# Half-turn of an 8192 x 8192 matrix by DMA alone: 128 rows a DMA in place of 32

## The chip, the cores and the metric

The kernel runs on one core of one Trainium2 chip. It computes nothing: it only issues DMAs that copy from one tensor in the chip's HBM (its main memory) to another. The core has 16 DMA engines that move the bytes, and two queues from which this kernel feeds them: the SP queue, filled by SyncE (SP), and the ACT queue, filled by ScalarE (ACT). In the profile's list of queues they are q1 (SP) and q10 (ACT).

The metric is the device time of one execution in microseconds (us), the median of several runs. A profile of one execution shows when each DMA was issued, when it landed, and how busy the DMA engines were.

## The reference

```python
x = np.random.randn(8192, 8192).astype(np.float32)
out = np.fft.ifftshift(x)
```

For even sizes this swaps the halves in both directions: `out[r, c] = x[(r + 4096) % 8192, (c + 4096) % 8192]`. The upper half of the rows changes places with the lower half, and inside each row the left 4096 floats change places with the right 4096. A row is 8192 floats, 32 KB; half a row is 16 KB. The tensor is 268.44 MB; all of it is read once and written once.

## The kernel before, in words

Output rows are copied in blocks of 32 neighbouring rows (`rows`, line 29), one DMA of 1 MB a block, 256 DMAs in all. No data passes through on-chip memory.

One DMA is described by two access patterns. The source pattern (`read`, line 35) is 16 pieces, each 64 KB long: two whole rows (`wide`, line 28), which lie one behind the other in memory. The destination pattern (`write`, line 36) walks 32 rows, and in each row two pieces of 16 KB: first the right half (offset `hc`), then the left half (a step of `-hc`). The bytes are taken from the source in order, so the left half of a source row lands in the right half of the output row, and the other way round. The source block begins 4096 rows further on, modulo 8192 (line 33). With 16 pieces of source and 16 DMA engines, a DMA is one 64 KB read and four 16 KB writes for each engine; an engine has two neighbouring rows.

The order is written out by hand by the two loops at lines 47 to 50. The outer loop takes parts of 1024 rows (`part`, 32 MB). In a part the SP queue works through the first 512 rows and the ACT queue through the last 512, each in blocks of `rows` in increasing order; the program issues one to SP and one to ACT by turns. So at every time the two queues work about 512 rows (16 MB) apart, and each is given 128 DMAs.

The DMAs are independent of each other. The framework around the kernel (the Tile context) gives each DMA a completion semaphore out of eight, four for each queue in turn. A DMA on a queue is therefore issued only when the fourth one before it on that queue has landed: at most four DMAs per queue, eight in all, are under way. These waits stand at line 37, where the instruction is added. At the end SP waits for the last ones (line 76, in the launch code).

Of the kernel before, what the change touches and what calls it, by code (L numbers as in the profile page):

```python
# [1 line left out]

# [4 lines left out]


ENGINES = 16


@with_exitstack
def kernel(
    ctx: ExitStack,
    tc: tile.TileContext,
    x: bass.AP,
    out: bass.AP,
):

    nc = tc.nc
    R, C = x.shape
    hr = R // 2
    hc = C // 2
    wide = 2
    rows = ENGINES * wide
    part = 1024  # L30

    def copy(queue, name, row):
        src = x.offset + (row + hr) % R * C
        dst = out.offset + row * C + hc
        read = [[wide * C, ENGINES], [1, 1], [1, wide * C]]
        write = [[C, rows], [-hc, 2], [1, hc]]
        queue.add_instruction(
            mybir.InstDMACopy(
                name=nc.get_next_instruction_name(),
                queue=name,  # L40
                mode="Copy",
                ins=queue.lower_ap_dma(bass.AP(x.tensor, src, read)),
                outs=queue.lower_ap_dma(bass.AP(out.tensor, dst, write)),
            )
        )

    for first in range(0, R, part):
        for row in range(first, first + part // 2, rows):
            copy(nc.sync, "qSPDynamicHW", row)
            copy(nc.scalar, "qActDynamicHW", row + part // 2)  # L50


# [1 line left out]
_INS = ['x']  # L54
_OUTS = [((8192, 8192), 'float32')]


# [23 lines left out]
```

## Time and profile before

| what | value |
|---|---|
| median of 3 runs | 821.62 us (821.31 to 823.12) |
| the profiled execution, its own time | 821.65 us |
| its span, first to last instruction | 819.9 us |
| bytes | 268.44 MB read, 268.44 MB written |
| mean rate over the span, read and written together | 655 GB/s |
| DMAs | 128 on SP, 128 on ACT, 1024 KB each |
| from the issue of a DMA to its landing, median | 25.5 us |

The span leaves out what lies around the first and last instruction, here 821.65 - 819.9 = 1.75 us. The page cuts the span into 40 slices of 20.5 us and gives for each the busy share of the 16 DMA engines in tenths (9 means 90% or more) and the rate in GB/s. That rate counts each byte once, by the writes; the reads are the same again. A "packet" in the list of queues is one write or one completion message. The packets of 16 KB are the writes of half rows; those under 512 B are the completion messages, one per engine and DMA (256 x 16 = 4096). A share of the DMA engines can be printed a little above 1.00 in a short stretch, since a packet is counted whole where it begins.

### The profile page before, as it was taken

Reading aid. Unit: us, or ns where it says so; the run is one execution under the profiler, and the core shown is the slowest. Engines: PE = TensorE matmul, PEld = TensorE weight load, DVE = VectorE, ACT = ScalarE, POOL = GpSimd, SP = SyncE. Lnnn points to the kernel's source line nnn. Section 1 sums busy time; section 2 is a strip of 40 time slices with the busy share of each in tenths; the row PEclk is TensorE's granted clock in tenths of the full one; section 3 lists DMA queues with packets and bytes.
Section 4 is the critical chain, followed back from the end, with each engine's and each line's share of the span. In section 5 each row is a group of like instructions: output and inputs, shape, how many; then the busy total and the mean of one; then the engine's idle time right before and its main releaser. Section 6 shows DMA issues by size and latency. Waiting matters only on the chain. (4 is left out here: it accounts for less than half of the span.)

```text
span 819.9 us, 301 instructions
## 1 busy us (share of the span) xinstructions
POOL 0.2 (0%) x4
## 2 busy tenths in 40 slices
POOL 0000000000000000000000000000000000000000
DMA  9999999999999999999999999999999999999998
GB/s 301 329 327 330 323 331 333 323 333 330 325 333 331 331 329 324 333 332 327 331 328 329 331 329 334 329 332 328 333 320 325 330 328 333 327 335 326 329 325 294
DMA packets 20483, 268.47 MB, mean 327 GB/s; under 512 B 4097, under 2 KB 4097, under 8 KB 4097
## 3 DMA queue, kind: packets, MB, share of 16 engines
q1 hardware_dynamic: 10240, 134.23, 50.1%
q10 hardware_dynamic: 10240, 134.23, 49.3%
q14 instruction: 3, 0.02, 0.0%
HBM read 268.44 MB, written 268.44 MB: 655 GB/s over the span
## 5 line engine op out<-in xcount | busy, mean ns | idle before, releaser
L65 POOL MEMSET const-bfloat16-1.0<- 128x1 bf16 x1 | 0.1, 101 | 0.0
L65 POOL MEMSET const-uint8-127<- 128x1 uint8 x1 | 0.1, 101 | 0.0
L65 POOL MEMSET const-float32-0.0<- 128x1 f32 x1 | 0.1, 98 | 0.2 <-issue 0.2
L65 POOL MEMSET const-float32-1.0<- 128x1 f32 x1 | 0.1, 98 | 0.0
## 6 DMA issues: line engine op xcount, KB each, us to landing
out_dram<-in_x_dram ACTq DMA_DIRECT2D x128, 1024.0 KB, 25.5
out_dram<-in_x_dram SPq DMA_DIRECT2D x128, 1024.0 KB, 25.5
```

The costliest lines, as they stand in the source:

```text
L65: nc = _bacc.Bacc("TRN2", target_bir_lowering=False, num_devices=1)
```

## The change

A DMA covers 128 neighbouring rows in place of 32: 4 MB in place of 1 MB. The source pattern becomes 64 pieces of 64 KB, the destination pattern 128 rows of two halves. The size of a read (64 KB), the size of a write (16 KB), the two queues, the parts of 1024 rows, the order of rows and the framework's eight semaphores stay. There are 64 DMAs in place of 256, 32 on each queue; four blocks on each queue make up a part in place of sixteen.

```diff
     wide = 2
-    rows = ENGINES * wide
+    rows = ENGINES * 8
     part = 1024
 
     def copy(queue, name, row):
         src = x.offset + (row + hr) % R * C
         dst = out.offset + row * C + hc
-        read = [[wide * C, ENGINES], [1, 1], [1, wide * C]]
+        read = [[wide * C, rows // wide], [1, 1], [1, wide * C]]
         write = [[C, rows], [-hc, 2], [1, hc]]
```

If an engine is given a run of neighbouring pieces, it has four reads of 64 KB and sixteen writes of 16 KB a DMA: eight rows, 256 KB. The 16 engines then stand 256 KB apart in memory, where they stood 64 KB apart.

## The prediction

> **What bounds the kernel now.** I read the page from the top, then SP's waits, then the start, middle and end in stretches. First the page: span, slices, queues, issues.
>
> ```profile
> span 819.9 us, 301 instructions
> ...
> DMA  9999999999999999999999999999999999999998
> GB/s 301 329 327 330 323 331 333 323 333 330 325 333 331 331 329 324 333 332 327 331 328 329 331 329 334 329 332 328 333 320 325 330 328 333 327 335 326 329 325 294
> DMA packets 20483, 268.47 MB, mean 327 GB/s; under 512 B 4097, under 2 KB 4097, under 8 KB 4097
> ...
> q1 hardware_dynamic: 10240, 134.23, 50.1%
> q10 hardware_dynamic: 10240, 134.23, 49.3%
> ...
> out_dram<-in_x_dram ACTq DMA_DIRECT2D x128, 1024.0 KB, 25.5
> out_dram<-in_x_dram SPq DMA_DIRECT2D x128, 1024.0 KB, 25.5
> ```
>
> The two queues' packets take 50.1 + 49.3 = 99.4% of the time of 16 engines: the engines are full from end to end, and only their pace can change the time. The 38 inner slices average 329.1 GB/s and lie between 320 and 335. A write of 16 KB takes 0.994 x 16 x 819.9 us / 16,384 = 796 ns. The list of SP's waits comes next.
>
> ```profile
> SPq L37 <- DMA out_dram<-in_x_dram: 722.6, 124, 8.7
> ```
>
> SP waits 722.6 us before 124 of its 128 issues, each time for an earlier DMA to land. This is not the bound: with eight DMAs of 1 MB under way a landing must take 8 x 821.65/256 = 25.7 us, and it takes 25.5. The queue in front of the engines is never empty. Last the stretches: start, end, us, GpSimd (POOL), clock, share of the DMA engines, GB/s.
>
> ```profile
> 0.00:2.00 2.00, 0.20 (x4) 1.00 0.00 0
> 2.00:5.00 3.00, 0.00 (x0) 1.00 0.96 339
> ...
> 100.00:700.00 600.00, 0.00 (x0) 1.00 1.00 329
> ...
> 815.00:820.00 5.00, 0.00 (x0) 1.00 0.55 180
> ```
>
> Nothing moves for 2.0 us at the start, and in the last 5 us the engines are 45% idle (2.25 us). At 329.1 GB/s the 268.44 MB alone take 815.7 us; the other 821.65 - 815.7 = 5.95 us are these ends and what lies around the span. The median of the runs, 821.62, is the same as the profiled 821.65, so sums against the latter need no correction.
>
> **The change part by part.**
>
> *Fewer DMAs, so fewer seams.* 192 of 256 DMAs go, with three quarters of the completion packets. Idle time of the engines is 0.6% of 819.9 = 4.9 us; the ends explain 2.0 + 2.25 = 4.25, which leaves 0.65 us for all seams together. The completion packets also take engine time: 9 ns each in the packet records behind these views, 256 x 9 ns = 2.3 us per engine. Three quarters of both is 0.5 + 1.7 = 2.2 us. That is the most that can be gained here; the least is 0, because an engine held up by memory loses nothing by a 9 ns message. I take 0.5, the idle part alone.
>
> *Fewer issues.* An issue takes 553 to 560 ns, up to 820 at the start, in the durations of line 37; a queue's 128 of them make 71 us, all beside the transfers, since SP has 722.6 us to wait. Gain 0. If an issue grows with the number of pieces (four times 560 is 2.2 us), it is still hidden behind three DMAs of 4 MB on its queue. Only the first, 642 ns on ACT, is uncovered: 0 to 3 x 0.64 = 1.9 us. Issues of like size all take the same, so no row decides; I take 0, as the pieces can leave while the issue runs on.
>
> *The waits* go from 124 to 28 per queue, for landings four times as long (8 x 4 MB, some 103 us). Behind the waiting issue on SP and on ACT stand only later issues of the same queue. 32 MB are under way in place of 8, so no engine runs dry: 0.
>
> *The two ends.* The start's stretch is ACT's first DMA almost alone; SP follows. If ACT keeps its head start for sixteen writes an engine in place of four, SP is alone for as long at the end. One queue alone is not slower (339 GB/s in 2 to 5 us against 329), so 0. If the engines end four times as far apart, the 2.25 us idle at the end become 9: 0 to +6.8. I take 0: nothing makes an engine drift further because messages are rarer, as the waits do not hold the engines together now either.
>
> *The places in memory.* This is the term that decides. The 16 engines keep near step with each other. Now they stand 64 KB apart and cover one solid megabyte; afterwards they stand 256 KB apart over 4 MB. Sizes and order within an engine are the same. That memory, or the way to it, sets the pace can be seen: the same 16 KB write takes from 609 to over 1300 ns in the packet records, 796 on average. 0.61 us x 1024 writes per engine would be 625 us. So some 190 us are waiting, which the arrangement of addresses can raise or lower. No row shows another spacing. The nearest rows are the slices, which differ in address alone: the slowest, 320 GB/s, would make 838.9 us for the bytes (+23.2), the fastest, 335, 801.3 (-14.4). I take a loss: engines over one solid megabyte differ in every address bit from 64 KB up; at 256 KB they share two more bits at any moment, which can only put more of them on the same part of the memory, unless higher bits are mixed in. For its size I take the mean of the lower 19 slices, 326.4 GB/s: 822.4 us for the bytes, +6.7, since the extremes are single slices of 20.5 us.
>
> The Trainium skill bears on both sides. "DMA: Bandwidth & Descriptors", section "Measured (HBM→SBUF, 128 partitions, SWDGE, issued from GpSimd)", says to batch DMAs to at least 1 MiB and has larger ones faster still: 341 GB/s at 1 MB, 425 at 16 MB. By those two figures four times the size would, as an estimate from that page, gain up to a fifth; but they are loads into SBUF, and the share of 1.00 in the stretch from 100 to 700 us says that the fixed cost of a DMA is already covered here by the other seven. I give such a gain no more than what is left below the range. The same page, "Latency and other measured facts", reports copies between HBM tensors losing rate as the row pitch grows through large powers of two: 207 GB/s at 512 KiB, 103 at 4 MiB, against 214 with padding. Its lowest pitch is above our 256 KB; if the 3.4% between 214 and 207 held here, the estimate would be 849 us. No run so far shows which part of that table applies to engines 256 KB apart.
>
> The sum: 821.65 - 0.5 + 6.7 = 827.9, so 828.
>
> **The rivals.**
>
> *No effect of the places (821).* Only the seams count: 821.65 - 0.5 = 821.1, bounds 819.4 (all 2.2 gained) and 823.5 (a first issue four times as long). For it: the rate stays within 320 to 335 whatever rows are being copied, as if addresses were well mixed. Against it: even those slices differ by 4.6%, and all have the same spacing.
>
> *The places help (about 814).* This is the other side: with 190 us of waiting, if 16 engines side by side in one megabyte collide now, engines 256 KB apart collide less. At the mean of the upper 19 slices, 331.8 GB/s, the bytes take 809.0 and the whole 809.0 + 5.95 - 0.5 = 814.5; at 335 it is 806.8. It decides as soon as the rate passes 329.6 GB/s, where the sum is 0.2% below now. For it: the waiting is large. Against it: nothing shows that neighbours collide, and solid coverage is the more even spread.
>
> *The engines drift apart (828).* No change of pace, but the end stretched by 6.8 us and no gain at the seams that shows: 821.1 + 6.8 = 827.9. For it: each engine has 4 MB / 16 of its own to finish after the last issue. Against it: the last 5 us still have 55% of the engines busy, so they end close together though eight DMAs under way would allow 25 us.
>
> *The change does not do what it says.* The 64 pieces could be dealt one by one, so that engines stay 64 KB apart. Then only the seams are left: 821.1.
>
> **How the numbers follow.** Dearer places 0.42, forecast 828; drift 0.08; no effect 0.18 and pieces dealt one by one 0.06, both near 821; cheaper places 0.26. The runs of before differ by about 0.2% (1.6 us), which is also what a measurement of this kernel can tell from no change. Slower is 0.42 + 0.08 = 0.50. Of the 0.24 near 821, 0.03 fall below -0.2% by a full gain at the seams: same 0.21. Faster is 0.26 + 0.03 = 0.29. The range goes down to 808, about the fastest slice's 806.8, and up to 850: the slowest slice's 821.65 - 0.5 + 23.2 = 844 and most of a drift of 6.8 on top. The forecast's own range, of dearer places alone, is 823.5 to 850. Outside the whole range I leave 0.06 below and 0.09 above.
>
> **What would show it.** 64 issues of 4096 KB, landings of about 103 us, 28 waits on SP, 1024 completion packets and 16,384 writes: then the change is as described. The inner slices near 326 GB/s with the share of the engines still 9 in every slice: the places. Slices unchanged and a lower last one: the drift. Slices at 332 or more: the forecast is wrong because the waiting came from neighbours. Slices in the middle with a share under 9 would mean that engines ran dry, which no step here allows for.

## The result

| | before | after |
|---|---|---|
| median of 22 runs each | 821.82 us (820.97 to 823.12) | 822.99 us (822.01 to 824.14) |
| span of the profiled execution | 819.9 us | 821.4 us |

The ratio is 1.0014, with a 95% interval from 1.0008 to 1.0020. The kernel became 1.2 us slower: a real difference, but a fifth of the 6.3 us that was forecast, and below the 0.2% that the prediction counted as a change. It lies within the bounds of the rival "no effect of the places" (821.1, bounds 819.4 to 823.5).

The page after the change, the lines that answer to those of before:

```profile
span 821.4 us, 109 instructions
...
DMA  9999999999999999999999999999999999999999
GB/s 302 325 326 326 323 326 329 333 334 332 324 330 330 329 322 327 332 331 326 327 332 331 326 329 323 329 328 330 326 333 330 327 327 328 331 326 331 323 328 301
DMA packets 17408, 268.44 MB, mean 327 GB/s; under 512 B 1024, under 2 KB 1024, under 8 KB 1024
...
q10 hardware_dynamic: 8704, 134.22, 49.8%
q1 hardware_dynamic: 8704, 134.22, 49.7%
...
out_dram<-in_x_dram ACTq DMA_DIRECT2D x32, 4096.0 KB, 102.1
out_dram<-in_x_dram SPq DMA_DIRECT2D x32, 4096.0 KB, 102.0
```

By its counts the change did what it says: 64 issues of 4096 KB, 1024 completion packets, 16,384 writes, landings after 102 us where 103 were worked out. The engines are still full (49.8 + 49.7 = 99.5%). The inner 38 slices average 328.2 GB/s against 329.1, and lie between 322 and 334. That the engines now stand 256 KB apart cannot be read from this page; the run with 512 rows a DMA below bears it out.

SP's waits, and the stretches at the start, in the middle and at the end (start, end, us, GpSimd, clock, share of the DMA engines, GB/s):

```profile
SPq L37 <- DMA out_dram<-in_x_dram: 697.8, 28, 25.6
```

```profile
2.00:5.00 3.00, 0.00 (x0) 1.00 0.99 333
...
100.00:700.00 600.00, 0.00 (x0) 1.00 1.00 329
...
816.50:821.50 5.00, 0.00 (x0) 1.00 0.57 190
```

28 waits, as forecast. The middle moves 329 GB/s as before. The last five microseconds have a share of 0.57 where they had 0.55, so the engines did not drift apart. The completion messages in the trace say the same: the last of the 16 engines finishes its part of a DMA 1.2 us after the first (median), where it was 1.4 us. By the slices, the bytes take 268.44 MB / 328.2 GB/s = 817.9 us, 2.2 more than before, and what lies around them in the profiled execution (823.16 us) shrinks from 5.95 to some 5.2 us. Single slices scatter by several GB/s, so this split of a difference of 1.5 us is rough.

### The profile page after: what moved, and what is told of

Its sections match the earlier page's. It is cut to its first block, busy times and chain, and to the rows that moved or that the text cites. A ratio compares the mean times of both kernels' runs of the same rounds, so it can differ in the third digit from the quotient of the medians.

```text
span 821.4 us, 109 instructions
## 1 busy us (share of the span) xinstructions
POOL 0.2 (0%) x4
## 2 busy tenths in 40 slices
DMA packets 17408, 268.44 MB, mean 327 GB/s; under 512 B 1024, under 2 KB 1024, under 8 KB 1024
## 3 DMA queue, kind: packets, MB, share of 16 engines
q10 hardware_dynamic: 8704, 134.22, 49.8%
q1 hardware_dynamic: 8704, 134.22, 49.7%
HBM read 268.44 MB, written 268.44 MB: 654 GB/s over the span
```

## The experiments

The question was why a change of spacing from 64 KB to 256 KB, forecast to cost 6.7 us, costs next to nothing. Either spacing does not matter at all, or a loss from spacing and a gain from fewer seams nearly cancel, or it matters only further out.

To vary the spacing without varying the DMAs, the next runs give each engine one row per DMA: 16 rows, 512 KB, with a free distance `apart` between the engines' rows. Their common edit:

```diff
-        read = [[wide * C, ENGINES], [1, 1], [1, wide * C]]
-        write = [[C, rows], [-hc, 2], [1, hc]]
+        read = [[apart * C, ENGINES], [1, 1], [1, C]]
+        write = [[apart * C, ENGINES], [-hc, 2], [1, hc]]
...
-        for row in range(first, first + part // 2, rows):
-            copy(nc.sync, "qSPDynamicHW", row)
-            copy(nc.scalar, "qActDynamicHW", row + part // 2)
+        for base in range(first, first + part // 2, ENGINES * apart):
+            for row in range(base, base + apart):
+                copy(nc.sync, "qSPDynamicHW", row)
+                copy(nc.scalar, "qActDynamicHW", row + part // 2)
```

The reads can be cut in this way without a change of their size: in the instructions as they are built, before and after the change, the framework cuts the source to the pieces of the destination.

```
before   source [[4096, 64], [1, 1], [1, 4096]]    destination [[8192, 32], [-4096, 2], [1, 4096]]
after    source [[4096, 256], [1, 1], [1, 4096]]   destination [[8192, 128], [-4096, 2], [1, 4096]]
```

In these lists each pair is a step and a count, in floats: the source is pieces of 4096 floats, 16 KB. So a read is issued as 16 KB pieces and not, as the source text and the text ahead of the prediction have it, as 64 KB. The change does not touch this.

**Twice the seams, same places** (`apart = 2`).

> One row per engine and DMA, engines 64 KB apart as before: the same addresses in the same order as the kernel before, in 512 DMAs of 512 KB in place of 256 of 1 MB, so twice the completion packets (8192). Theory A, the engines wait for memory and a completion packet fits into that waiting: 821 to 823 us, no change. Theory B, completion packets cost engine time one for one (9 ns each, 256 more per engine = 2.3 us, and 0.65 us of seams doubled): 821.8 + 3.0 = 824.8 us; then the change gained some 2.2 us by fewer packets and lost some 3.4 us by its places.

Measured: 822.46 us, 1.0006 times before (0.9997 to 1.0014). The slices of its page:

```profile
GB/s 303 326 326 326 330 326 331 328 326 334 327 331 328 334 328 326 334 326 332 329 325 330 327 333 332 329 330 327 328 331 327 332 326 329 331 326 332 327 330 275
```

256 more completion packets per engine cost at most 0.0014 x 821.9 = 1.15 us. Theory B's 3.0 us are excluded, which fits Theory A: the packets mostly go into time in which the engine waits anyway. So the change had little to gain from fewer seams, and no loss of 3.4 us by the places was hidden behind a gain.

**Engines 256 KB apart** (`apart = 8`).

> As the run with one row per engine and DMA, but the engines stand 256 KB apart, as after the change; number and size of the DMAs are those of that run. Theory A, spacing up to 256 KB does not matter: within 0.2% of the run with engines 64 KB apart. Theory B, the places cost some 3.4 us: 0.4% above it. The prediction's dearer places: 6.7 us, 0.8% above it.

Measured on the same chip: 822.84 us, 1.0012 times before (1.0004 to 1.0021). The difference to the run with 64 KB is 0.4 us, and the two intervals overlap. The 6.7 us of the prediction are excluded: from the lowest end of the one interval, 0.9997, to the upper end of the other, 1.0021, it is 2.0 us.

**Engines 8 MB apart** (`apart = 256`, with `part = 8192`, so that the two queues are half a matrix apart).

> As the run with one row per engine and DMA, but the engines stand 8 MB apart (256 rows), so that an engine has a sixteenth of each queue's half of the matrix to itself. If addresses are well mixed at all distances: within 0.5% of the run with engines 64 KB apart. If the distance between engines in step does matter, only further out than 256 KB: clearly slower. As an estimate from the Trainium skill, DMA: Bandwidth & Descriptors, section Latency and other measured facts (103 against 214 GB/s at a pitch of 8 MiB): about twice the time, 1700 us.

Measured: 3032 us, in single runs from 2890 to 3084. Even the fastest is 3.5 times before. The page of this run:

```profile
span 3057.5 us, 557 instructions
...
DMA  6889699668997898998879697798788789898987
GB/s 89 87 81 89 84 86 86 88 88 90 86 82 84 86 83 89 83 88 85 85 88 85 91 88 86 91 92 91 87 92 91 89 92 96 88 92 92 90 93 82
```

The rate is 81 to 96 GB/s throughout, and a share below 9 in many slices says that engines stand idle at times. A DMA lands after 47.7 us (median), which is what eight DMAs always under way make: 8 x 3057.5 / 512 = 47.8. By its completion messages the last engine finishes its part of a DMA 8.7 us after the first (median), against 1.4 us before. So engines that are done wait for others that hold up the eight DMAs. In this run the queues' distance grew too, from 16 MB to 128 MB, and it was not varied by itself. Even so, spacing matters very much; it only does not matter yet at 256 KB.

**512 rows a DMA.**

```diff
-    rows = ENGINES * 8
+    rows = ENGINES * 32
```

> The change carried on: 512 rows, 16 MB a DMA, 16 DMAs, engines 1 MB apart, 256 completion packets in all. Theory A: 822 to 824 us, as after the change. Theory B (seams gain, places cost): another 0.4 us of packets gained and a further loss by the spacing, some 826 us. If the small loss of the change lies at the ends of the run, where whole DMAs are larger: it grows with the size of a DMA, to 826 us or more, with the inner slices unchanged.

Measured: 1101 us, 1.340 times before (1.335 to 1.344). No theory had this. It is not the ends, since the inner slices fall from some 328 GB/s to between 222 and 258:

```profile
GB/s 221 252 249 253 232 240 250 246 255 232 234 253 255 249 235 222 252 255 250 236 243 250 253 252 231 240 248 249 257 233 244 251 249 248 243 235 258 252 253 208
```

But in this run the size of a DMA and the distance between engines (1 MB) grew together, so three more distances were measured with small DMAs.

**Engines 512 KB apart** (`apart = 16`).

> One row per engine and DMA, engines 512 KB apart (16 rows). Theory A, the distance between engines in step is what costs, from some distance on: the first distance at which it shows lies between 256 KB (822.84) and 1 MB; between 823 and 1100 us, and the inner slices show it evenly. Theory B, only very large DMAs cost, not the distance: 822 to 823 us.

Measured: 872.16 us, 1.061 times before (1.059 to 1.062).

**Engines 1 MB apart** (`apart = 32`).

> One row per engine and DMA, engines 1 MB apart (32 rows), DMAs of 512 KB. Theory A, the distance made the run with 512 rows a DMA slow: about 1100 us, inner slices near 245 GB/s. Theory B, the size of its DMAs made it slow (16 MB each, 64 writes per engine): 822 to 823 us here.

Measured: 1125.5 us, 1.368 times before (1.363 to 1.373). DMAs of 512 KB are as slow as DMAs of 16 MB (1101 us) when the engines stand 1 MB apart. It is the distance and not the size. This also speaks against the prediction's rival that the pieces are dealt one by one: then the engines of the run with 512 rows would have stood close together, and it would hardly be as slow as the run that sets them 1 MB apart. The middle of these runs, one fence each; first 256 KB:

```profile
100.00:700.00 600.00, 0.00 (x0) 1.00 1.00 329
```

Then 512 KB:

```profile
100.00:600.00 500.00, 0.00 (x0) 1.00 1.00 310
```

And 1 MB:

```profile
100.00:700.00 600.00, 0.00 (x0) 1.00 1.00 240
```

The share is 1.00 in all three: the engines are always at work, and each write takes longer. The busy share alone would show no difference between them; the GB/s beside it does.

**1 MB and 64 KB apart** (34 rows).

```diff
+    half = R // 2
+    starts = [(b + r, 34) for b in range(0, 7 * 544, 544) for r in range(34)]
+    starts += [(b + r, 2) for b in range(7 * 544, half, 32) for r in range(2)]
...
+    for row, apart in starts:
+        copy(nc.sync, "qSPDynamicHW", row, apart)
+        copy(nc.scalar, "qActDynamicHW", row + half, apart)
```

> As the run with engines 1 MB apart, but 34 rows (1 MB and 64 KB) apart; the last 288 rows of each half are done with engines 64 KB apart, and the two queues work half a matrix apart. If it is the distance as such that costs: about 1100 us. If it is that all engines agree in the address bits below 1 MB: the extra 64 KB makes them differ, and it goes back to 822 to 826 us.

Measured: 925.3 us, 1.125 times before (1.121 to 1.129). A larger distance, but two thirds of the loss are gone: 200 of 303 us. So the greater part of the loss does not come from the distance as such. The likely reading is that it comes from engines that agree in the address bits below 1 MB, since the extra 64 KB makes just these differ. The other third stays, though below 1 MB the engines now stand as in the kernel before; what it comes from is not shown. The queues' distance grew here as well, to 128 MB, and was not varied by itself.

**One queue.**

```diff
-    part = 1024
...
-    for first in range(0, R, part):
-        for row in range(first, first + part // 2, rows):
-            copy(nc.sync, "qSPDynamicHW", row)
-            copy(nc.scalar, "qActDynamicHW", row + part // 2)
+    for row in range(0, R, rows):
+        copy(nc.sync, "qSPDynamicHW", row)
```

> The DMAs of the kernel before, 32 rows each, all on the SP queue, row after row; four under way in place of eight, and one place in the matrix in place of two. If the two queues' places collide with each other, or more places at a time cost: faster, down to the 625 us that 0.61 us a write would give. If one queue leaves gaps: slower, with a share of the DMA engines under 1.00. If the pace is the memory's whatever the queues: 820 to 825 us.

Measured: 823.34 us, 1.0006 times before (0.9997 to 1.0015). Its slices:

```profile
GB/s 300 328 329 328 333 322 329 333 326 329 325 327 325 331 325 335 323 329 329 334 325 323 328 330 335 332 326 330 327 332 324 323 333 325 329 336 330 326 329 285
```

Half the DMAs under way, and one place in the matrix in place of two: no difference. What sets 329 GB/s is not a matter of the queues.

**Writes alone.** One load of 2 MB, then only writes from on-chip memory, as many and as large as before, in DMAs of 2 MB:

```diff
+    held = pool.tile([2 * rows, hc], mybir.dt.float32)
+    nc.sync.dma_start(out=held[:], in_=x[0:rows].rearrange("r (h c) -> (r h) c", h=2))
...
+        to = out[row : row + rows].rearrange("r (h c) -> (r h) c", h=2)
+        queue.dma_start(out=to, in_=held[:])
```

> The reads from HBM are taken away: 2 MB of x are loaded once into on-chip memory, and every DMA writes these to 64 output rows, in writes of 16 KB; the output is not the half-turn. If the 796 ns of a write hold waiting for memory that reads and writes share: writes near 0.61 us, 1024 of them per engine, about 635 us with the load. If the engines cannot write faster than this whatever they read: about 820 us.

Measured: 642.2 us, one run. The slices of its page:

```profile
GB/s 311 426 426 426 430 428 425 428 428 426 431 426 428 426 426 426 426 426 426 426 426 426 426 426 426 426 426 426 426 429 426 427 427 426 429 427 426 430 429 377
```

Without the reads from HBM such writes go at a steady 426 GB/s, 16 x 16,384 B / 426 GB/s = 0.615 us a write, which is next to the shortest write in the kernel before (608 ns). The 180 us between this and the kernel before come with the reads from HBM.

Are the reads alone so slow? The load at the start of this run reads 2 MB from HBM and writes none. Of its 128 packets of 16 KB, 106 took 608 to 615 ns, the others up to 1839 while it began, and once it is under way it moves 431 GB/s:

```profile
4.00:7.00 3.00, 0.00 (x0) 1.00 1.01 431
```

So far as 2 MB can tell, neither the reads nor the writes alone are held up; reading and writing HBM at the same time is. Whether the memory itself or the way to it is the narrow place, no run shows. And no spacing tried, from 32 KB to 256 KB, takes any of these 180 us away.

**Engines 32 KB apart** (`apart = 1`).

> One row per engine and DMA with the engines 32 KB apart (16 neighbouring rows, 512 DMAs). If what holds the pace at 329 GB/s still contains collisions that come from the distance: a little faster than the run with 64 KB, under 821 us. If the distance costs nothing up to 256 KB because something else sets the pace: 822 to 823 us.

Measured: 824.16 us, 1.0031 times before (1.0012 to 1.0050). Closer is not better; it is slightly worse, and its single runs scatter more (821.8 to 832.3); why is not shown. No kernel tried that copies the whole matrix beats the kernel before.

**Only the reads, only the writes 1 MB apart.** For each queue the two sides take the same number of rows in a different order:

```diff
+    froms, tos = 32, 2        # the other run: 2, 32
...
+        read = [[froms * C, ENGINES], [1, 1], [1, C]]
+        write = [[tos * C, ENGINES], [-hc, 2], [1, hc]]
```

> The reads with engines 1 MB apart, the writes with engines 64 KB apart; so rows land in other places than the half-turn's. 822 us is both near, 1125 us both far. If reads carry the cost: near 1100; if writes do: near 830; if both: between, about 950.

Measured: 905.2 us, one run.

> The writes with engines 1 MB apart, the reads with engines 64 KB apart; rows land in other places than the half-turn's. If writes carry the cost: near 1100 us; if reads do: near 830; if both: between, about 950.

Measured: 952.8 us, one run. Both sides pay, the writes somewhat more (130 us against 83 over the 822.5 with both near). Together, at 1125.5, they cost 303 us, more than the sum of 213.

In one table, all with 16 rows a DMA. The runs were made on three chips, on which the kernel before takes 821.9 to 822.7 us, so that differences of about 1 us between rows of the table say nothing. In the last two rows the queues stand 128 MB apart and not 16 MB.

| distance between engines | time, us | over 64 KB, us |
|---|---|---|
| 32 KB | 824.2 | +1.7 |
| 64 KB (places of before) | 822.5 | |
| 256 KB (places of after) | 822.8 | +0.4 |
| 512 KB | 872.2 | +50 |
| 1 MB | 1125.5 | +303 |
| 1 MB + 64 KB | 925.3 | +103 |
| 8 MB | 3032 | +2210 |

## Why the prediction was wrong

*What bounds the kernel* was right: the engines are full from end to end in every copy up to 1 MB, and only their pace moves the time.

*Fewer issues, the waits, the two ends*, all taken at 0: right. The landings take four times as long, SP waits 28 times, an issue takes 552 to 560 ns as before though it has four times the pieces, the start moves 333 GB/s in 2 to 5 us, and the last stretch has a share of 0.57 against 0.55. The bound of +6.8 us for engines that drift apart was not needed.

*Fewer seams*, -0.5 us within 0 to -2.2: right in kind. The reason given for the lower bound, that an engine held up by memory loses nothing by a 9 ns message, fits what doubling the messages showed. In the run after the change the idle part went from 4.9 us to 0.5% x 821.4 = 4.1 us, and 1.7 us of messages an engine went away. Both came back as longer writes: in the packet records the mean write went from 793.7 to 797.8 ns, which is 4.2 us over an engine's 1024 writes. (The prediction's 796 ns holds the messages too.)

*The places in memory*, +6.7 us, is the step that failed, and it failed in its size. Measured in isolation it is +0.4 us, not distinguishable from 0, and at most 2.0 us. Two parts of its working were wrong. First, the price was taken from the scatter of the slices, read as the effect of different addresses. But a slice mean of 320 to 335 GB/s appears again with one queue (322 to 336), with twice the seams (325 to 334) and after the change (322 to 334), whichever rows are copied. The run with twice the seams copies the same rows in the same order as the kernel before, and yet its slow and fast slices lie elsewhere: slice by slice the two pages have a correlation of 0.06. So the slices show how much 20 us of this traffic scatter, not how addresses act. The slower half of any such scatter lies below its mean, so this way of pricing gives a loss whatever a change does. Second, the 190 us of waiting in the writes were taken as something that the arrangement of addresses "can raise or lower". The run with writes alone shows that they come with reading and writing at once. Reads and writes together move some 2 x 329 = 658 GB/s with one queue or two and at every distance from 32 KB to 256 KB, so this looks like a common ceiling. Collisions of a small size may take place under it and not show; that is not tested.

A loss from a larger distance between engines in step does exist (the engines finish a DMA within 1.4 us of each other before the change). It is far larger than was allowed for, and begins between 256 and 512 KB: the change stops one step short of it. That it comes from shared address bits, as the prediction argued, fits the two thirds that 64 KB more won back, and is not shown for the rest. The prediction noted a condition, "unless higher bits are mixed in", and had no row to say at which distance the loss begins.

The Trainium skill's page "DMA: Bandwidth & Descriptors", section "Latency and other measured facts", was the better guide to the form of the curve than the slices: it has little loss at a row pitch of 512 KiB and half the rate at 4 and 8 MiB. The runs agree in kind and differ in size: for the distance between engines, which need not be the page's row pitch, they have 310 GB/s at 512 KB, 240 at 1 MB and some 88 at 8 MB, against 329. The page's cure of some KiB of padding was not tried as it stands; 64 KB on 1 MB took away two thirds of the loss. The batching rule of the same page of the Trainium skill, section "Measured (HBM→SBUF, 128 partitions, SWDGE, issued from GpSimd)", by which larger DMAs go faster, finds no support here: 1 MB, 4 MB and 512 KB a DMA at 64 to 256 KB all lie within 0.2%.

What the remaining +1.2 us are (by the interval +0.7 to +1.6) stays open. The run with small DMAs 256 KB apart has +0.9 over before (1.0004 to 1.0021), so the places may account for them; but the run with the old places in small DMAs has +0.6, and no run tells these apart. That the time moved in the forecast's direction therefore does not speak for its mechanism.

## What to carry to other kernels

When a DMA is made larger by giving each engine a longer run, the distance between the engines grows with it, and that distance has a cliff: here nothing that can be told from noise up to 256 KB, 6% at 512 KB, 37% at 1 MB, and 3.5 times the time or more at 8 MB. Keep the engines' simultaneous places close; where they must be far apart, an odd 64 KB on top of 1 MB won back two thirds in the one run that tried it. Do not take a busy share of 1.00 for a sign that nothing is lost: look at the GB/s beside it. Before pricing a wait, find what it waits for by taking one side away; the run with writes alone tells that some 180 of the 190 us go when the reads go. And do not price an effect by the slower half of a scatter before a second run has shown that the same slices are slow again.

## What was not expected

- The size of the effect of distance. From 64 KB to 8 MB between the engines, with the same bytes and DMAs of the same size, the time goes from 822.5 to 3032 us. The page of the run at 8 MB also shows idle engines in its inner slices, which no other run has.
- Reads and writes of HBM together are held at 655 GB/s, where the writes alone reach 426. Neither the number of queues (823.3 us with one) nor the bytes under way (4 MB with one queue or with 512 KB DMAs, 32 MB after the change) move this. The Trainium skill's "HBM Reference", section "Specifications (TRN2)", gives some 716 GB/s for the memory of a pair of cores; by that figure, as an estimate, 655 is 91% of it, so a ceiling of the memory itself may be the cause, but no run here shows that it is this one.
- Spacing on both sides at once costs more (303 us) than on the reads (83) and the writes (130) added, each of these two from one run.
